# Turning attention probabilities by DMA transposes of 16-bit halves instead of TensorE transposes, for five of sixteen pairs of heads

## The chip, the cores and the metric

The kernel runs on one core of one Trainium2 chip. The metric is the device time of one execution in microseconds; the median of the two runs shown is 601.02 us (600.94 and 601.1). The core has five engines that run side by side, each in its own program order: TensorE (PE, with its weight loads PEld), VectorE (DVE), ScalarE (ACT), GpSimd (POOL) and SyncE (SP, which here only issues DMAs). They wait for one another by semaphores.

## The reference

One layer of a hybrid diffusion trunk: 1024 latent tokens and 128 prompt tokens of width 1024, in float32. After a normalised, modulated input projection there are two groups of heads. The part that the change touches is the attention of the latent tokens, which read 1024 latent keys and 256 cached context keys in one softmax:

```python
def one_block(i):
    s0 = i * Q_BLOCK
    qn = lax.dynamic_slice_in_dim(q_nope, s0, Q_BLOCK, axis=1)
    logits = []
    for qr, (kn, kr, _) in zip(q_ropes, key_sets):
        qrb = lax.dynamic_slice_in_dim(qr, s0, Q_BLOCK, axis=1)
        logits.append(jnp.einsum('bqhn,bkhn->bhqk', qn, kn)
                      + jnp.einsum('bqhr,bkr->bhqk', qrb, kr))
    s = jnp.concatenate(logits, axis=-1).astype(jnp.float32) * ATTN_SCALE
    p = jax.nn.softmax(s, axis=-1).astype(v_all.dtype)
    return jnp.einsum('bhqk,bkhv->bqhv', p, v_all)
```

The group's output is gated, joined with the other group's, multiplied by the output projection w_o, added to the input under a gate and normalised.

## The kernel before

The kernel is one stream of stages: modulation and input projections (to about 315 us of the span), attention (to about 510 us), output projection and normalisation (to the end). Matmuls are done in three passes on float32 values split into a high part (rounded to float32r by ScalarE or GpSimd) and a low part (the rest, a subtraction on VectorE: lo_of, line 112).

**Attention.** There are 8 tiles of 128 queries and 4 heads, in 16 pairs of heads (pair 0 is tile 0, heads 0 and 1; pair 6 is tile 3, heads 0 and 1; pair 10 is tile 5, heads 0 and 1). The loop at line 2006 runs over c. In iteration c, TensorE does the scores of pair c + 1 (score_steps, line 1511) and, woven into them, the value products of pair c - 1 (value_steps, line 1593). A score-only stretch and a value stretch are merged by planned costs (merged, line 212), so that TensorE always has the one while the other's helpers work.

For one head, scores lie in PSUM as 128 queries x 1280 keys (tile s, two buffers, one for each head of a pair). softmax (line 1453) takes maxima on VectorE (L1463 over 1024 columns, L1466 over 256), exponentials on ScalarE into e (L1481), and lets GpSimd multiply e by 1/sum (L1486). The value product contracts over keys, so e must be turned: tr(i) (L1609) transposes four 128x128 blocks of e on TensorE into a PSUM tile pT, five times for a pair (10 blocks of keys x 2 heads). ScalarE copies pT rounded into ph (L1613), VectorE subtracts to get pl (L112), and av(i) (L1633 to L1635) multiplies ph and pl by the values, with tr two steps ahead of av (LAG). e has 6 buffers, ph and pl 4 each, os (the copied value sum) 2.

**Who else works there.** In iterations up to c = 9 GpSimd also forms sums of w_o blocks in tile traw (t_unit, line 1921; L790, four subtractions in an iteration), ScalarE and VectorE split them (L1932, L112), and SP stores the pieces to a DRAM buffer tdram (L1928) and loads the next (L1919). From c = 10 on, SP loads whole pieces of w_o (wo_piece, line 1691; L1705) whose high part GpSimd makes (L115). The first five go through buffers of their own, the last three into buffers of e, so they wait until the turned e of an early enough head is read.

**What sets the order.** The order on each engine is written out: later(dt, fn) puts a piece of work into a list at a planned time, and need(key) runs the list on until that work has been written. No engine reorders anything; if a helper is late, the instructions behind the waiting one on the same engine are late too.

## Time and profile before

| | |
|---|---|
| median of the runs | 601.02 us |
| profiled execution | 600.68 us |
| its span (first to last instruction) | 598.9 us |
| PE busy in the span | 588.7 us (98%) |
| DVE, ACT, POOL busy | 428.7, 329.7, 213.5 us |
| mean granted TensorE clock | 0.997 |
| DMA | 67.33 MB, mean 112 GB/s |

The profiled execution's time is 1.8 us above its span: what lies around the first and last instruction. It is 0.34 us below the median of the runs.

A row of the timeline gives start, duration, engine, line, operation, tiles written and read, and shapes; "x4" merges four. Matmul durations overlap, as the array is pipelined: what one costs is the distance to the next start. The attention iterations of the middle begin, by the first score matmul of each, at 370.0, 381.9, 393.7, 405.6, 417.5, 429.3, 441.2, 453.0 and 464.8 us of the span; these are c = 5 to c = 13.

### The profile page before, as it was taken

How to read it: one execution, taken by the hardware profiler on the slowest of the kernel's cores; microseconds unless marked ns; L12 is line 12 of the kernel's file. 1: busy time of each engine (PE TensorE's matmuls, PEld its weight loads, DVE VectorE, ACT ScalarE, POOL GpSimd, SP SyncE). 2: the span in 40 equal slices, each digit the busy share in tenths (PEclk: the TensorE clock that was granted, in tenths of full speed). 3: DMA queues.
4: the chain of work that ended last, by engine and by line, in shares of the span. 5: the costliest groups of instructions: out<-in, count | busy, mean ns of one | idle time of the engine just before them, and what ended most of it. 6: DMA issues, size and time to landing. Idle time of an engine off the chain costs nothing.

```text
span 598.9 us, 10175 instructions
## 1 busy us (share of the span) xinstructions
PE 588.7 (98%) x3653; PEld 527.0 (88%) x3653; DVE 428.7 (72%) x946; ACT 329.7 (55%) x771; POOL 213.5 (36%) x251
## 2 busy tenths in 40 slices
PE   8999999999999999999999999999999999999995
PEld 7578889999999999999998888888888898888884
DVE  3676888967647467476678677778788876477885
ACT  6665886434323245455567556655756462457543
POOL 2562103200000000343264345454543547269834
PEclk9999999999999999999999999999999999999998
DMA  8991002051050134100002033434242019951444
GB/s 314 366 378 74 1 4 68 1 210 71 7 207 26 45 96 138 42 1 0 2 8 71 0 106 111 156 123 142 85 144 90 1 71 307 359 178 39 140 153 161
DMA packets 31059, 67.33 MB, mean 112 GB/s; under 512 B 3344, under 2 KB 17440, under 8 KB 29984
## 3 DMA queue, kind: packets, MB, share of 16 engines
q1 hardware_dynamic: 27792, 55.93, 26.7%
q0 software_dynamic: 2352, 8.39, 4.1%
q10 hardware_dynamic: 864, 2.36, 1.2%
q8 instruction: 29, 0.48, 0.3%
q14 instruction: 22, 0.18, 0.1%
HBM read 53.45 MB, written 13.21 MB: 111 GB/s over the span
## 4 chain that ended last, share of the span: by engine, by line
PE 92%; DMA 3%; POOL 2%; DVE 1%; ACT 1%; issue 0%; SPq 0%; POOLq 0%; ACTq 0%
PE p L928 15%; PE tp L949 7%; PE pT L1609 5%; PE o L1633 3%; PE o L1635 3%; PE o L1634 3%; PE zacc L1372 2%; PE zacc L1371 2%; PE zacc L1373 2%; PE S L1970 2%; PE S L1971 2%; PE S L1972 2%; DMA ada<-in_ada_ss 2%; PE s L1526 2%; PE s L1529 2%; PE s L1528 2%
## 5 line engine op out<-in xcount | busy, mean ns | idle before, releaser
L1486 POOL TENSOR_SCALAR e<-e,rs 128x1280 f32<-128x1280 f32 x32 | 47.0, 1470 | 96.8 <-DVE rs L1485 64.7
L112 DVE TENSOR_TENSOR pl<-pT,ph 128x512 fp32r<-128x512 f32 x81 | 55.5, 686 | 32.8 <-ACT ph L1613 32.6
L1481 ACT ACTIVATE e<-s,nb,scl 128x256 f32<-128x256 f32 x64 | 56.9, 891 | 38.8 <-DVE nb L1469 26.2
L1613 ACT CAST ph<-pT 128x512 fp32r<-128x512 f32 x80 | 47.2, 590 | 40.6 <-PE pT L1609 40.3
L1219 POOL TENSOR_TENSOR kr<-z,rope 128x64 f32<-128x64 f32 x8 | 2.6, 326 | 154.6 <-ACT z L1228 154.6
L949 PE MATMUL tp<-area,w 128*128 128x384 f32 x288 | 52.5, 337 | 0.0
L1633 PE MATMUL o<-ph,vh 128*128 128x256 f32 x160 | 50.7, 317 | 0.0
L949 PEld LDWEIGHTS tp<-area,w 128*128 128x128 f32 x288 | 50.4, 188 | 0.0
L1609 PE MATMUL pT<-ident,e 128*128 128x128 f32 x320 | 47.9, 272 | 0.0
L1609 PEld LDWEIGHTS pT<-ident,e 128*128 128x128 f32 x320 | 38.9, 140 | 7.2
L1635 PE MATMUL o<-ph,vl 128*128 128x256 f32 x160 | 45.1, 282 | 0.0
L1634 PE MATMUL o<-pl,vh 128*128 128x256 f32 x160 | 44.8, 280 | 0.0
L1463 DVE TENSOR_REDUCE m<-s 128x1 f32<-128x1024 f32 x32 | 38.9, 1216 | 2.6 <-PE s L1504 2.5
L1633 PEld LDWEIGHTS o<-ph,vh 128*128 128x128 f32 x160 | 30.2, 188 | 4.7 <-ACT os L1643 2.9
L1634 PEld LDWEIGHTS o<-pl,vh 128*128 128x128 f32 x160 | 30.3, 189 | 0.4
L1635 PEld LDWEIGHTS o<-ph,vl 128*128 128x128 f32 x160 | 30.1, 188 | 0.0
L928 PE MATMUL p<-area,w 128*128 128x384 f32 x144 | 27.6, 337 | 0.0
L928 PE MATMUL p<-area,s 128*128 128x384 f32 x144 | 27.3, 337 | 0.0
L1371 PE MATMUL zacc<-w1t,area 128*128 128x448 f32 x72 | 27.0, 375 | 0.0
L928 PE MATMUL p<-w1t,s 128*128 128x384 f32 x144 | 26.6, 339 | 0.0
L1372 PE MATMUL zacc<-w1t,area 128*128 128x448 f32 x72 | 26.3, 366 | 0.0
L1373 PE MATMUL zacc<-w1t,area 128*128 128x448 f32 x72 | 26.3, 365 | 0.0
(703 smaller groups left out, 1767.8 us busy)
## 6 DMA issues: line engine op xcount, KB each, us to landing
ada<-in_ada_ss SPq DMA_DIRECT2D x16, 512.0 KB, 8.6
w2r<-in_w_t SPq DMA_DIRECT2D x12, 512.0 KB, 5.3
x<-in_x SPq DMA_DIRECT2D x9, 512.0 KB, 5.6
adag<-in_ada_g SPq DMA_DIRECT2D x4, 1024.0 KB
traw<-in_w_o SPq DMA_DIRECT2D x16, 256.0 KB, 3.0
tdram<-thi SPq DMA_DIRECT2D x32, 128.0 KB, 1.8
tdram<-traw SPq DMA_DIRECT2D x32, 128.0 KB, 1.8
wor<-in_w_o SPq DMA_DIRECT2D x8, 512.0 KB, 3.8
```

What stands on the lines that cost most here:

```text
L112: V.tensor_tensor(lo, src, f32(hi), op=ALU.subtract)
L928: T.matmul(banks[key], a_, b_, start=k == 0 and m == 0, stop=k == 3 and m == len(passes) - 1)
L949: T.matmul(tps[c, 2][:, :GW], w_[c][:, k, :], x_[k, 2], start=k == 0 and m == 0, stop=k == NK - 1 and m == 2)
L1371: T.matmul(ps[:, :448], a, wqh[k], start=k == 0, stop=False)
L1463: V.tensor_reduce(m[:, 0:1], lat_, axis=AX.X, op=ALU.max)
L1481: S.activation(e[:, sl], src, AF.Exp, bias=nb, scale=scl[:, t : t + 1], accum_out=su[:, i : i + 1])
L1486: G.tensor_scalar(e, e, rs, 0.0, op0=ALU.mult, op1=ALU.add)
L1609: T.transpose(ps[:, w : w + P], es[t, h][:, c * P : (c + 1) * P], ident)
L1613: later(0.5, lambda: S.copy(ph[:, :w], ps[:, :w]))
L1633: T.matmul(o, vh[:, kt, :], ph[:, sl], start=c == 0, stop=False)
L1634: T.matmul(o, vh[:, kt, :], pl[:, sl], start=False, stop=False)
L1635: T.matmul(o, vl[:, kt, :], ph[:, sl], start=False, stop=c == n - 1)
```

## The change

For the pairs in CONV, 6 to 10, e is no longer turned on TensorE. When GpSimd has normalised a head's e, it copies e twice more, as 16-bit integers: once the low and once the high halves of the 32-bit words, gathered into a tile b of 128 x 2 x 1280 (to_dram). SP stores b to a DRAM buffer pd. In the next iteration SP issues two DMA transposes of 512 rows x 640 columns of 2 bytes for the pair (from_dram). Since the rows alternate low and high half, the halves of a word stand side by side again after the turn, in a tile raw in SBUF, 128 keys x 10 blocks x 256 queries of two heads in float32. parts(i) then makes ph and pl from raw instead of from pT.

The value products of these pairs move one iteration back: those of pair 6 from c = 7 to c = 8, and so on; those of pair 10 come to c = 12, ahead of those of pair 11. Iteration c = 7 has none. To make room, e goes from 6 to 5 buffers, ph and pl from 4 to 3, os from 2 to 1. raw lies where the first two pieces of w_o went, so their loads move from after the last t_unit to the end of c = 12, behind pieces 2 to 4.

```diff
+CONV = range(6, 11)
...
+    pdram = [gd.tile([2, P, 2, 1280], U16, tag=f"pd{i}", name=f"pd{i}") for i in range(2)]
...
+    def to_dram(t, h):
+
+        both = ap_.tile([P, 1280], F32, tag="b", name=f"b{t}{h}", bufs=2).bitcast(U16).rearrange("p (s c) -> p s c", s=2)
+        words = es[t, h].bitcast(U16).rearrange("p (c s) -> p s c", s=2)
+        for i in range(2):
+            pool_copy(both[:, i, :], words[:, i, :])
+
+        def store():
+            nc.sync.dma_start(pdram[(2 * t + h // 2) % 2][h % 2], both)
+            made.add(("st", t, h))
+
+        later(5.2, store)
+
+    def from_dram(p_):
+        need(*[("st", *pairs[p_][:1], 2 * pairs[p_][1] + x) for x in range(2)])
+        if "raw" not in turned:
+            turned["raw"] = ht.tile([P, 6144], F32, tag="area0", name="raw0")
+        raw = turned[p_] = turned["raw"][:, 2560 * (p_ % 2) : 2560 * (p_ % 2) + 2560]
+        dst = raw.bitcast(U16).rearrange("p (c r) -> p c r", c=10)
+        rows = pdram[p_ % 2].rearrange("h q s c -> (h q s) c")
+        for i in range(2):
+            nc.sync.dma_start_transpose(dst[:, 5 * i : 5 * i + 5, :], rows[:, 640 * i : 640 * i + 640])
...
-        e = ap_.tile([P, 1280], F32, tag="e", name=f"e{t}{h}", bufs=6)
+        e = ap_.tile([P, 1280], F32, tag="e", name=f"e{t}{h}", bufs=5)
...
             made.add(("e", t, h))
+            if 2 * t + h // 2 in CONV:
+                to_dram(t, h)
...
         def tr(i):
+            if 2 * t + pr in CONV:
+                return parts(i)
...
+        def parts(i):
+            src = turned[2 * t + pr][:, 512 * i : 512 * i + 512]
+            ph, pl = pts[i] = tuple(ap_.tile([P, 512], F32R, tag=n_, name=f"{n_}{t}{pr}_{i}", bufs=3) for n_ in ("ph", "pl"))
+            S.copy(ph, src)
+
+            def low():
+                lo_of(pl, src, ph)
+                made.add(("p", t, pr, i))
+
+            later(0.65, low)
...
-            steps.append((0.44, lambda i=i: it[1](i)))
+            steps.append((0.0 if pairs.index(pair) in CONV else 0.44, lambda i=i: it[1](i)))
...
+            if c - 1 in CONV:
+                later(2.0, lambda c=c: from_dram(c - 1))
...
-                merged(sc, value_stream(pairs[c - 1]) if c > 0 else [])
+                merged(sc, [s_ for p_ in range(c) if p_ + 1 + (p_ in CONV) == c for s_ in value_stream(pairs[p_])])
...
+            if c == CONV[-1] + 2:
+                weights_room()
```

GpSimd, at the two heads of pair 6 (e30, e31), before; traw are the w_o blocks, a pair of subtractions to a row:

```order
L1486 TENSOR_SCALAR e30_4251<-e30_4251,rs30_4250 128x1280
L790 TENSOR_TENSOR traw3_4094<-traw3_4094 128x256 x2
L1486 TENSOR_SCALAR e31_4302<-e31_4302,rs31_4301 128x1280
L790 TENSOR_TENSOR traw4_4256<-traw4_4256 128x256 x2
L1486 TENSOR_SCALAR e32_4414<-e32_4414,rs32_4413 128x1280
```

and after:

```order
L1514 TENSOR_SCALAR e30_4253<-e30_4253,rs30_4252 128x1280
L117 TENSOR_SCALAR b30_4325<-e30_4253 128x1280 x2
L793 TENSOR_TENSOR traw3_4096<-traw3_4096 128x256 x2
L1514 TENSOR_SCALAR e31_4304<-e31_4304,rs31_4303 128x1280
L117 TENSOR_SCALAR b31_4399<-e31_4304 128x1280 x2
L793 TENSOR_TENSOR traw4_4258<-traw4_4258 128x256 x2
L1514 TENSOR_SCALAR e32_4423<-e32_4423,rs32_4422 128x1280
```

Two copies stand between a head's normalisation and the w_o subtractions, and so ahead of the next head's normalisation.

SP in the same place, before; thi and traw are the split w_o blocks on their way to DRAM:

```order
L1928 DMA tdram_92<-traw3_4094 128x256 x2
L1928 DMA tdram_92<-thi31_4387 128x256 x2
L1928 DMA tdram_92<-traw3_4094 128x256 x2
L1919 DMA traw5_4419<-in_w_o 128x2x256 x2
L1928 DMA tdram_92<-thi40_4521 128x256 x2
```

and after; pd0 is the DRAM buffer of pair 6, raw0 the tile that its transposes fill:

```order
L1971 DMA tdram_92<-thi31_4392 128x256 x2
L1466 DMA pd0_93<-b30_4325 128x2560
L1971 DMA tdram_92<-traw3_4096 128x256 x2
L1962 DMA traw5_4428<-in_w_o 128x2x256 x2
L1466 DMA pd0_93<-b31_4399 128x2560
L1479 DMA_TRANSPOSE raw0_4524<-pd0_93 128x5x512 x2
L1971 DMA tdram_92<-thi40_4527 128x256 x2
```

The two stores and the two transposes stand in the one queue with the w_o stores, which follow them.

TensorE at the start of iteration c = 7 before: a block of scores of pair 8 (s140), then the turning of pair 6 (pT30), then value products left from pair 5 (o2):

```order
L1526 MATMUL s140_4493<-kch_3227,area1_119 128x512
L1527 MATMUL s140_4493<-kcl_3228,area1_119 128x512
L1528 MATMUL s140_4493<-kch_3227,area1_119 128x512
L1529 MATMUL s140_4493<-krh_3229,area1_119 128x512
L1609 MATMUL pT30_0_4501<-ident_75,e30_4251 128x128
L1609 MATMUL pT30_0_4501<-ident_75,e31_4302 128x128
L1633 MATMUL o2_4259<-ph21_3_4446,vh_3231 128x256
L1634 MATMUL o2_4259<-pl21_3_4447,vh_3231 128x256
```

and after, from the context scores of head 0 (s2) over the halves of both heads (L1563) to head 1 (s141):

```order
L1530 MATMUL s2_3388<-kch_3229,area1_121 128x256
L1531 MATMUL s2_3388<-kcl_3230,area1_121 128x256
L1532 MATMUL s2_3388<-kch_3229,area1_121 128x256
L1533 MATMUL s2_3388<-krh_3231,area1_121 128x256
L1534 MATMUL s2_3388<-krl_3232,area1_121 128x256
L1563 MATMUL s140_4506<-krl_3232,area1_121 128x512
L1563 MATMUL s141_4531<-krl_3232,area1_121 128x512
L1556 MATMUL s141_4531<-kch_3229,area1_121 128x512
```

Iteration c = 7 is scores alone now; the left value products of pair 5 follow in c = 8, behind the first scores of pair 9.

More of the change, by code (lines that the diff above doesn't have):

```diff
@@ L13 @@
 I32 = mybir.dt.int32
+U16 = mybir.dt.uint16
 AF = mybir.ActivationFunctionType
@@ L1956, in open_wo, with weights_room @@
             c_wo, wo = opened("wo", side="left")
+        def weights_room():
+            whole[0] = ht.tile([P, 16, GW], F32R, tag="area0", name="area0b").rearrange("p a c -> p (a c)")
+            flat[0] = [whole[0][:, n * 1024 : (n + 1) * 1024] for n in range(6)]
             for k in range(2):
```

15 lines of the change are left out of this document (8 added, 7 removed).

## The prediction

> **What bounds the kernel now.** I read the page's totals and chain first, then the windows of the attention iterations, then the timelines of single engines.
>
> ```profile
> span 598.9 us, 10175 instructions
> PE 588.7 (98%) x3653; PEld 527.0 (88%) x3653; DVE 428.7 (72%) x946; ACT 329.7 (55%) x771; POOL 213.5 (36%) x251
> PE 92%; DMA 3%; POOL 2%; DVE 1%; ACT 1%; issue 0%; SPq 0%; POOLq 0%; ACTq 0%
> core 0: us, PE busy (x) PEld busy (x) DVE busy (x) ACT busy (x) POOL busy (x), PEclk, DMA share, GB/s
> 393.75:405.62 11.87, 11.87 (x87) 10.49 (x85) 9.03 (x21) 7.42 (x17) 5.85 (x6) 1.00 0.29 98
> 441.20:453.00 11.80, 11.80 (x86) 10.42 (x85) 10.38 (x23) 6.59 (x14) 5.30 (x6) 1.00 0.37 134
> ```
>
> TensorE is the bound: 92% of the chain, and no gap in an iteration of 11.87 us at full clock. So work taken off it counts in full, until a helper is the slower one. VectorE has 9.03 us to do in an iteration, GpSimd 5.85.
>
> **What leaves TensorE.** In the timeline of TensorE (start, duration, engine, line), one step of turning with the value products behind it:
>
> ```profile
> 403.20 0.39 PE L1527 MATMUL s<-kcl,area 128*128 128x512 f32 x1
> 403.43 0.39 PE L1528 MATMUL s<-kch,area 128*128 128x512 f32 x1
> ...
> 403.88 0.60 PE L1609 MATMUL pT<-ident,e 128*128 128x128 f32 x4
> ...
> 404.55 0.28 PE L1635 MATMUL o<-ph,vl 128*128 128x256 f32 x1
> 404.67 0.28 PE L1633 MATMUL o<-ph,vh 128*128 128x256 f32 x1
> ...
> 405.03 0.28 PE L1500 MATMUL s<-kch,area 128*128 128x256 f32 x1
> L1609 PE MATMUL pT<-ident,e 128*128 128x128 f32 x320 | 47.9, 272 | 0.0
> ```
>
> From 403.88 to 405.03 are 1.15 us. Six value matmuls at the distance 0.12 (404.55 to 404.67) take 0.70 of them, so a step of four transposes costs 0.45. The 320 of the group are 16 pairs x 5 steps x 4; five pairs lose 25 steps: **-11.2 us**. That is 1.9%, so even a change without any cost stays just inside the 2% that a measurement of this kernel can tell from no change.
>
> **The empty iteration, c = 7.** It holds only scores: 16 matmuls at 0.23 (403.20 to 403.43), 10 at 0.12 and the halves of 0.66, so 5.5 us. But each head of the next pair needs the score buffer that the same head of the last pair frees with its exponential:
>
> ```profile
> 410.86 0.73 PE L1533 MATMUL s<-krl,area 64*128 64x512 f32 x4
> 416.81 0.20 ACT L1481 ACTIVATION_READ_ACCUMULATOR e<-s,nb,scl 128x1 f32 x1
> 417.37 0.28 PE L1504 MATMUL s<-krl,area 128*128 128x256 f32 x1
> 421.75 0.20 ACT L1481 ACTIVATION_READ_ACCUMULATOR e<-s,nb,scl 128x1 f32 x1
> ```
>
> Head 0 is complete with the halves at 411.5 and its buffer free at 417.0, 5.5 us later; head 1 is complete at 417.5 and free at 421.95, 4.5 later. Now the value products between cover this. Without them the halves of c = 7, due 2.4 us after its start (eight matmuls of 0.23, five of 0.12), wait until 4.5: 2.1 lost. c = 7 then ends 7.6 after its start (4.5 + 0.66 + 2.4), while head 0's buffer is free at 10.65 (5.15 + 5.5), and the first scores of c = 8 stand ahead of any value product: 3.0 more. Between 0, if the helpers, without pT to read, free the buffers that much sooner, and 5.1: I take **+4**, near the measured latencies.
>
> So, by TensorE alone, c = 12 would start at 393.7 + 5.5 + 4 + 4 x 9.6 (11.87 less five steps) = 441.7, where it was 453.0; c = 12 holds the values of pair 10 as well and takes 4.1 us more (0.7 and the rest of its five steps).
>
> **GpSimd.** Its rows in one iteration, and VectorE's beside the second e:
>
> ```profile
> 382.54 1.34 POOL L1486 TENSOR_SCALAR e<-e,rs 128x1280 f32<-128x1280 f32 x1 [3.26 <-DVE rs L1485]
> 383.84 1.56 POOL L790 TENSOR_TENSOR traw<-traw 128x256 f32<-128x256 f32 x2
> 388.01 1.62 POOL L1486 TENSOR_SCALAR e<-e,rs 128x1280 f32<-128x1280 f32 x1 [2.61 <-PE s L1533]
> 389.60 1.56 POOL L790 TENSOR_TENSOR traw<-traw 128x256 f32<-128x256 f32 x2
> 387.73 0.69 DVE L112 TENSOR_TENSOR traw<-traw,thi 128x512 fp32r<-128x512 f32 x1
> L115 POOL TENSOR_SCALAR area<-wor 128x512 fp32r<-128x512 f32 x12 | 7.3, 624 | 3.9 <-DMA wor<-in_w_o 3.9
> L790 POOL TENSOR_TENSOR mixB<-mixA 128x512 f32<-128x512 f32 x4 | 5.2, 1301 | 0.0
> ```
>
> A copy of 1280 16-bit integers is in no row. By elements it is like e's 1.34, same operation and count. By bytes it is 640 floats, 0.75 by the L115 row. Were it as slow per element as a subtraction of two tiles (1.301 for 512), it would take 3.25. I take 1.34. A pair then needs 2 x 1.34 + 4 x 0.78 + 4 x 1.34 = 11.2 us.
>
> The second e takes 1.62, beside a VectorE subtraction with both inputs in SBUF: 0.28 more. An iteration has two such now (traw). The change adds five, as pl is made from raw and ph, both in SBUF, where it was pT in PSUM. So a pair costs GpSimd 11.7 in c = 5 and 6, and 13.1 from c = 8. From 382.5 its queue ends with pair 6 at 394.2, pair 7 (due at 394.4) at 406.1, pair 8 at 419.2, pair 9 at 432.3, pair 10 (its second head has no w_o subtractions, -1.6) at 443.8. ScalarE (L1932) and SP's stores wait behind it; behind L1932 on ScalarE stand exponentials and ph, so TensorE is slowed before the data are missed.
>
> **Store and transposes.** Each is 640 KB (128 x 2560 x 2 bytes; 512 x 640 x 2 bytes).
>
> ```profile
> GB/s 314 366 378 74 1 4 68 1 210 71 7 207 26 45 96 138 42 1 0 2 8 71 0 106 111 156 123 142 85 144 90 1 71 307 359 178 39 140 153 161
> wor<-in_w_o SPq DMA_DIRECT2D x8, 512.0 KB, 3.8
> kvg<-in_kv_g SPq DMA_DIRECT2D x1, 64.0 KB, 6.8
> ```
>
> At the w_o load's rate 640 KB take 4.75 us. A transpose is in no row: between 1.7 (378 GB/s, the busiest slice) and 68 (ten times the 64 KB load of 6.8, the slowest for its size). I take 4.75, nearest to it in size and shape. Pair 10's first half then is there at 443.8 + 2 x 4.75 = 453.3. It is needed one us after c = 12 starts, as leftovers of pair 9 come first. So c = 12 starts at 452.3, not 441.7: **+10.6**, in which the helpers' waits of c = 8 to 11 are contained. With no collisions and the same copies the queue ends at 437.5, and the term is 4.3; with copies of 0.75 it is 0. On one queue SP moves the w_o stores and loads behind these DMAs; the loads are an iteration ahead and tdram is read from 495 on, so I cost that at nothing; if GpSimd is over 11 us late, that cover is gone and its own subtractions wait.
>
> The Trainium skill (VectorE: DVE Perf Modes, section The three transpose paths) gives 1309 ns for one 128 x 128 block of 2-byte values by DMA against 390 on TensorE; 20 blocks in turn would be an estimated 26 us. No run here shows it yet.
>
> **The end.** e has five buffers, so the w_o piece 6 now reuses one of pair 14's and waits with piece 7 for the last turning:
>
> ```profile
> 499.94 0.33 SPq L1705 DMA_DIRECT2D wor<-in_w_o x1
> 501.59 1.65 POOL L115 TENSOR_SCALAR krh<-wor 128x512 fp32r<-128x512 f32 x2
> 506.31 0.48 PE L1999 MATMUL w<-krh,area 128*128 128x512 f32 x1
> 507.17 1.21 POOL L115 TENSOR_SCALAR area<-wor 128x512 fp32r<-128x512 f32 x2 [3.93 <-DMA wor<-in_w_o]
> ```
>
> Piece 7, issued at 499.94, arrives at 507.17. Piece 6 (krh) would arrive then, be copied by 507.8 and split by 508.8, where TensorE uses it at 506.31: **+2.5**, between 0 (it comes sooner, with nothing ahead of it) and 5 (two pieces share the time). Three ph and pl suffice for two steps ahead, one os for a copy that TensorE reads before the next: nothing; if not, a step waits about 0.7.
>
> **Sum**, on the profiled execution's 600.7 (0.3 under the median): -11.2 + 4 + 10.6 + 2.5 = +5.9, **606.6 us**. With the GpSimd term between 4.3 and 16 (half way to that of the second rival) this case spans 600 to 612.
>
> **The rivals.**
>
> *GpSimd keeps up*: copies of 0.9 us or less, so that its pair fits into 9.6. Then VectorE, 10.38 us in the later window against 9.6, costs about 1, and the sum is -11.2 + 4 + 1 + 2.5 = -3.7: 597. For it: GpSimd's idle 6 us. Against it: e's 1.34 for as many elements. With a smaller hole and end it reaches 590.
>
> *The port is held whole* (slower). In another place a subtraction of SBUF tiles starts inside a GpSimd copy:
>
> ```profile
> 443.00 1.20 POOL L115 TENSOR_SCALAR area<-wor 128x512 fp32r<-128x512 f32 x2
> 443.65 1.10 DVE L112 TENSOR_TENSOR area<-wor,area 128x512 fp32r<-128x512 f32 x1 [0.62 <-POOL area L115]
> ```
>
> It takes 1.10, not 0.69, ending about 0.55 after the copy. If the two never run together, GpSimd's pair grows by all seven subtractions, 11.2 + 7 x 0.69 = 16.0 (12.5 in c = 5 and 6): its queue ends at 454.0, c = 12 starts at 462.5, +20.8 in place of 10.6: 617. It decides from about 14.7 a pair. Against it: e lost 0.28, not 0.69. The Trainium skill (SBUF — State Buffer, section SBUF: two separate sides) calls the port pair that VectorE and GpSimd share an exclusive lock for a whole instruction; by it the sum would be this rival's. The two rows above do not contradict it.
>
> *The transposes are slow* (slower). They follow one another on one queue: pair 6's can start at 399, pair 10's first is the ninth, so 399 + 9 x T must be 453: T up to 6.0 us hides behind GpSimd. Each us more costs 9: 615 at 7, 642 at 10. It also holds SP's other DMAs.
>
> *It costs nothing*: -11.2 and about 1 for VectorE, 590.5; only with no hole, or gaps that shrink, is it below 589.
>
> **Chances.** Forecast 0.37, GpSimd keeps up 0.27, port held whole 0.15, slow transposes 0.18, over 2% faster 0.03. Slower by over 2% (above 613): 0.12 of the port's, 0.17 of the transposes', 0.03 of the forecast's upper end, 0.32. Faster 0.03. Within 2% the rest, 0.65. The range of 593 to 628 leaves out the better part of the clean case (0.08) and transposes over 8.5 us (0.11).
>
> **What would show it.** Right: the group of turned pT has 220, not 320; TensorE idle in c = 7 and at the start of 8, waiting for ScalarE; the 16-bit copies near 1.34 and GpSimd over 90% busy from about 395 to 444; waits of ScalarE for traw and raw before c = 12; a gap before w<-krh near the end. Wrong: copies under 0.9 and no wait for raw (GpSimd keeps up), pl from raw at over 1.2 us each (port), or raw's DMAs landing over 6 us after issue with SP waiting on them (transposes).

## The result, and the profile after

The changed kernel takes 640.04 us (median of 2 runs, 639.44 to 640.64) against 601.02: the ratio is 1.065, with a 95% interval of 1.063 to 1.067. The forecast was 606.6 us, with a range of 593 to 628. The change is slower by 39 us, and the forecast fell short by 33.

From the page of the changed kernel: span, busy times, the granted clock of TensorE by slices, the chain's shares, and two groups (busy us, mean ns of one, and behind the second bar the idle time ahead of the group and what ended it).

```profile
span 637.6 us, 10050 instructions
PE 595.4 (93%) x3553; PEld 527.9 (83%) x3553; DVE 436.8 (69%) x947; ACT 332.4 (52%) x771; POOL 243.4 (38%) x271
...
PEclk9999999999999999999999999887896999999999
...
PE 70%; DMA 12%; DVE 8%; POOL 3%; ACT 3%; issue 2%; SPq 2%; ACTq 0%; POOLq 0%
...
L1641 PE MATMUL pT<-ident,e 128*128 128x128 f32 x220 | 33.1, 273 | 0.0
L117 POOL TENSOR_SCALAR b<-e 128x1280 uint16<-128x1280 uint16 x20 | 27.2, 1378 | 17.9 <-DMA pd<-b 17.5
```

The 100 transposes are gone (220 in the group, not 320), and yet TensorE is busy 6.7 us longer than before. Its share of the chain falls from 92% to 70%; what comes in is first DMA (from 3% to 12%) and VectorE (from 1% to 8%). Two things show at once that no row of before had: GpSimd waits 17.5 us for the stores to free its two buffers b, and TensorE's granted clock drops in slices 26 to 31.

The windows of the changed kernel from the halves of one iteration to those of the next, c = 7 to 12 (columns: length and sum, then busy us of TensorE, its weight loads, VectorE, ScalarE, GpSimd, the granted clock, the DMA share and GB/s):

```profile
399.40:412.90 13.50, 10.70 (x49) 8.19 (x48) 9.76 (x19) 7.86 (x16) 10.46 (x10) 0.87 0.78 207
412.90:429.20 16.30, 11.67 (x65) 9.85 (x64) 9.06 (x17) 6.30 (x13) 11.41 (x10) 0.90 0.70 188
429.20:450.90 21.70, 12.88 (x65) 10.48 (x64) 10.52 (x23) 9.07 (x21) 11.51 (x10) 0.84 0.80 227
450.90:467.20 16.30, 13.32 (x65) 11.05 (x64) 10.79 (x18) 7.11 (x14) 11.30 (x9) 0.79 0.87 261
467.20:491.00 23.80, 15.56 (x91) 13.80 (x90) 13.82 (x24) 8.85 (x18) 8.54 (x9) 0.78 0.65 175
```

Each was 11.87 us before (the last now holds part of two pairs' value products). The five are 1.6, 4.4, 9.8, 4.4 and 11.9 longer, 32 of the 39 us together; the rest comes behind them. TensorE is idle for 27.5 us of these 91.6. What it is busy is also stretched by the clock: busy time times the missing share of the clock (10.70 x 0.13 + 11.67 x 0.10 and so on) gives an estimate of 11 us.

SyncE's queue in the changed kernel, the time between one pair's transposes and the next (start, duration with waiting, what):

```profile
420.70 6.20 SPq L1479 DMA_TRANSPOSE raw<-pd  x2
...
430.06 0.40 SPq L1466 DMA_DIRECT2D pd<-b  x1
430.55 1.40 SPq L1971 DMA_DIRECT2D tdram<-traw  x2
433.90 1.22 SPq L1962 DMA_DIRECT2D traw<-in_w_o  x2
435.17 0.60 SPq L1466 DMA_DIRECT2D pd<-b  x1
439.96 2.68 SPq L1479 DMA_TRANSPOSE raw<-pd  x1
```

The two transposes keep SyncE for 6.2 us. Then come w_o's stores and loads and the store of the next pair's first head, 8.2 us, with SyncE standing for two of them until the stores to tdram have landed. Then 0.6 for the second head's store, and 4.2 until it has landed and the next transposes can go. That is 19.3 us for a pair, where an iteration of TensorE was to be 9.6. The other pairs' transposes follow at distances of 20.4, 15.3 and 19.1 us.

Who waits for whom, in the changed kernel from 370 to 520 us (total, times, longest):

```profile
ACT thi L1975 <- POOL traw L793: 18.7, 5, 7.1
ACT ph L1660 <- DMA raw<-pd: 18.7, 4, 6.3
POOL b L117 <- DMA pd<-b: 17.5, 5, 7.2
...
PE s L1530 <- ACT e L1509: 12.2, 5, 5.4
```

ScalarE stands in order at w_o's thi and at ph; the exponentials behind them come late; TensorE waits for the score buffers that the exponentials free.

The chain of work that ended last goes, in the stretch of SyncE's rows above, through these transfers (start, time until landing or until what they held up went on):

```profile
420.70 5.71 DMA raw<-pd
431.01 2.83 DMA tdram<-traw
435.17 4.78 DMA pd<-b
439.96 6.25 DMA raw<-pd
```

Between the first two stand ScalarE's ph, exponentials and VectorE's pl; between the next two the reload of traw, which must wait until the old piece is stored, and which stands ahead of the store of b in SyncE's queue. From 395 to 490 us the landing of the stores of b, of the transposes and of w_o's stores makes 22, 18 and 6.5% of the chain, 44 us of the 95.

### The profile page after: what moved, and what is told of

Its sections match the earlier page's. It is cut to its first block, busy times and chain, and to the rows that moved or that the text cites. A ratio compares the mean times of both kernels' runs of the same rounds, so it can differ in the third digit from the quotient of the medians.

```text
span 637.6 us, 10050 instructions
## 1 busy us (share of the span) xinstructions
PE 595.4 (93%) x3553; PEld 527.9 (83%) x3553; DVE 436.8 (69%) x947; ACT 332.4 (52%) x771; POOL 243.4 (38%) x271
## 4 chain that ended last, share of the span: by engine, by line
PE 70%; DMA 12%; DVE 8%; POOL 3%; ACT 3%; issue 2%; SPq 2%; ACTq 0%; POOLq 0%
PE p L931 14%; PE tp L952 7%; DMA pd<-b 3%; DMA raw<-pd 3%; PE pT L1641 2%; PE zacc L1375 2%; PE zacc L1374 2%; PE zacc L1376 2%; PE S L2018 2%; DMA ada<-in_ada_ss 2%; DVE pl L114 2%; PE S L2019 2%; PE S L2017 2%; DVE m L1491 2%; PE o L1676 2%
## 5 line engine op out<-in xcount | busy, mean ns | idle before, releaser
L114 DVE TENSOR_TENSOR pl<-pT,ph 128x512 fp32r<-128x512 f32 x56 | 38.2, 685 | 22.1 <-ACT ph L1645 22.0
L1645 ACT CAST ph<-pT 128x512 fp32r<-128x512 f32 x55 | 32.3, 588 | 33.1 <-PE pT L1641 32.0
L1677 PE MATMUL o<-pl,vh 128*128 128x256 f32 x160 | 46.4, 290 | 0.0
L1676 PEld LDWEIGHTS o<-ph,vh 128*128 128x128 f32 x160 | 31.8, 199 | 15.3 <-ACT os L1686 13.2
L117 POOL TENSOR_SCALAR b<-e 128x1280 uint16<-128x1280 uint16 x20 | 27.2, 1378 | 17.9 <-DMA pd<-b 17.5
L114 DVE TENSOR_TENSOR pl<-raw,ph 128x512 fp32r<-128x512 f32 x25 | 19.8, 794 | 19.7 <-ACT ph L1660 19.5
L1641 PE MATMUL pT<-ident,e 128*128 128x128 f32 x220 | 33.1, 273 | 0.0
L1641 PEld LDWEIGHTS pT<-ident,e 128*128 128x128 f32 x220 | 26.4, 140 | 4.9 <-issue 0.4
L1530 PE MATMUL s<-kch,area 128*128 128x256 f32 (+2 forms) x52 | 18.1, 349 | 12.2 <-ACT e L1509 12.2
L1660 ACT CAST ph<-raw 128x512 fp32r<-128x512 f32 x25 | 15.3, 616 | 25.4 <-DMA raw<-pd 18.7
L1556 PE MATMUL s<-kch,area 128*128 128x512 f32 x48 | 22.3, 465 | 6.2 <-ACT e L1509 6.1
```

The lines of the kernel that those rows point to most:

```text
L114: V.tensor_tensor(lo, src, f32(hi), op=ALU.subtract)
L117: G.tensor_scalar(out, in_, 1.0, 0.0, op0=ALU.mult, op1=ALU.add)
L1641: T.transpose(ps[:, w : w + P], es[t, h][:, c * P : (c + 1) * P], ident)
L1645: later(0.5, lambda: S.copy(ph[:, :w], ps[:, :w]))
L1676: T.matmul(o, vh[:, kt, :], ph[:, sl], start=c == 0, stop=False)
L1677: T.matmul(o, vh[:, kt, :], pl[:, sl], start=False, stop=False)
```

## The experiments

Three theories stood at the start: **1**, SyncE's queue (the stores stand behind the transposes, the copies' buffers stay taken, GpSimd stops); **2**, the time that the data need through DRAM; **3**, the amount of GpSimd's work, as the prediction had it. Theories 4 and 5 came from the runs: **4**, the place of the copies in GpSimd's order; **5**, a ring through SyncE's queue (a pair's transposes, w_o's stores, the next pair's stores and their landing) that sets the pace. Ratios are to the kernel before, run on the same chip.

### The parts one by one

**The cuts alone.** No pair is converted; the fewer buffers and the later w_o pieces stay.

```diff
-CONV = range(6, 11)
+CONV = ()
-            if c == CONV[-1] + 2:
+            if c == 12:
```

> No pair is converted; only the buffers are those of the changed kernel (five e, three ph and pl, one os) and the w_o pieces 0 and 1 are loaded at c = 12. This is the price of the cuts alone: the prediction has 2.5 us at the end (0 to 5), so 603.5, between 601 and 606; more than 608 would mean that the missing buffers, and not the DMAs, cost part of the 39 us.

Measured 604.45 us, ratio 1.006 (1.004 to 1.008). The iterations are as before and the loss lies behind them. The buffers are not what costs 39 us.

**The empty iteration alone.** TensorE turns all pairs, but the value products of pairs 6 to 10 come an iteration later. Two pairs' e lie in the idle area0 for it; e, ph, pl and os have their old number of buffers.

```diff
+        if 2 * t + h // 2 in (8, 10):
+            e = turned["raw"][:, 1280 * n_ : 1280 * n_ + 1280]
-            if 2 * t + h // 2 in CONV:
-                to_dram(t, h)
-            if 2 * t + pr in CONV:
-                return parts(i)
-            if c - 1 in CONV:
-                later(2.0, lambda c=c: from_dram(c - 1))
```

> The kernel before, with TensorE's transposes, but the value products of pairs 6 to 10 come one iteration later, as in the changed kernel: c = 7 holds scores alone and c = 12 two pairs' values. No copies, stores or DMA transposes. What it costs over 601 is the hole alone: the prediction put 4 us on it, between 0 and 5.1, so 601 to 606. If the hole explains more (for instance by a lower granted clock after TensorE's pause), 608 or more with a clock below 1.00 behind c = 7.

Measured 612.02 us, ratio 1.019 (1.017 to 1.020): 11.2 us, more than the upper end, and with a lower clock. TensorE's timeline of this kernel in c = 7 and 8:

```profile
397.21 0.39 PE L1534 MATMUL s<-kch,area 128*128 128x256 f32 x1 [0.57 <-ACT e L1515]
...
398.91 0.73 PE L1567 MATMUL s<-krl,area 64*128 64x512 f32 x3 [0.43 <-ACT e L1515]
...
404.46 0.78 PE L1560 MATMUL s<-kch,area 128*128 128x512 f32 x1 [1.93 <-ACT raw L1515]
405.03 0.63 PE L1561 MATMUL s<-kcl,area 128*128 128x512 f32 x1
405.46 0.63 PE L1562 MATMUL s<-kch,area 128*128 128x512 f32 x1
...
408.45 0.39 PE L1561 MATMUL s<-kcl,area 128*128 128x512 f32 x1
408.68 0.39 PE L1562 MATMUL s<-kch,area 128*128 128x512 f32 x1
```

The waits are the predicted ones, for exponentials that free score buffers: 0.57, 0.43 and 1.93 us, 2.9 together. Behind the longest the matmuls come at a distance of 0.43 us (405.03 to 405.46), and four us later at 0.23 again. So the pause is paid for a second time in half the clock: what stands between 404.46 and 408.22 takes 3.8 us, and 2.1 by the distances at full clock. The windows of this kernel from the halves of c = 6 to those of c = 8, and from c = 11 to c = 13:

```profile
388.00:411.40 23.40, 20.46 (x115) 16.45 (x114) 14.80 (x36) 11.82 (x26) 11.17 (x12) 0.93 0.37 121
...
447.20:479.10 31.90, 30.77 (x225) 27.25 (x224) 23.25 (x45) 16.73 (x34) 11.00 (x11) 1.00 0.14 50
```

Twice 11.87 us, less the value products of one pair (11.87 - 5.5 = 6.4), would be 17.4; the first window takes 6.0 more. Twice 11.87 with the 6.4 added would be 30.1; the second takes 1.8 more. Some 2 us come at the end, as with the cuts; the rest is not located.

**The copies alone.** To the cuts, the 20 copies of 16-bit halves are added; nothing is stored, and TensorE turns all pairs.

```diff
-        def store():
-            nc.sync.dma_start(pdram[(2 * t + h // 2) % 2][h % 2], both)
-            made.add(("st", t, h))
-        later(5.2, store)
-            if 2 * t + h // 2 in CONV:
+            if 2 * t + h // 2 in range(6, 11):
                 to_dram(t, h)
```

> The kernel with the cuts alone (TensorE turns all 16 pairs, value products at their old place), with the 20 copies of 16-bit halves added on GpSimd for pairs 6 to 10 and nothing behind them: no stores, no transposes, nobody reads the copies. It prices GpSimd's load by itself, over 604.5 of the cuts alone. By the prediction's step (GpSimd 11.7 to 13.1 us a pair against iterations of 9.6) the queue must here fit into 11.87 us an iteration, so 1 to 6 us: 605 to 610. If GpSimd's load, through the waits of ScalarE for traw, is what makes most of the loss with plain loads (622), it shows here as 612 or more. If the stores and the order of SyncE's queue are it, 604 to 606.

Measured 617.7 us, ratio 1.027 (1.026 to 1.029): 13 us over the cuts. But GpSimd is not full. Its timeline, VectorE's, and three waits of this kernel (between 375 and 490 us):

```profile
412.89 2.48 POOL L117 TENSOR_SCALAR b<-e 128x1280 uint16<-128x1280 uint16 x2
415.33 2.04 POOL L793 TENSOR_TENSOR traw<-traw 128x256 f32<-128x256 f32 x2
417.86 1.34 POOL L1508 TENSOR_SCALAR e<-e,rs 128x1280 f32<-128x1280 f32 x1 [0.49 <-DVE rs L1507]
```

```profile
416.09 0.69 DVE L114 TENSOR_TENSOR traw<-traw,thi 128x512 fp32r<-128x512 f32 x1 [2.66 <-POOL traw L793]
416.70 0.69 DVE L114 TENSOR_TENSOR pl<-pT,ph 128x512 fp32r<-128x512 f32 x1
...
418.05 1.68 DVE L114 TENSOR_TENSOR traw<-traw,thi 128x512 fp32r<-128x512 f32 x1 [0.40 <-ACT thi L1969]
```

```profile
POOL e L1508 <- DVE rs L1507: 36.6, 16, 4.1
...
DVE traw L114 <- POOL traw L793: 10.3, 4, 2.7
ACT thi L1969 <- POOL traw L793: 9.1, 5, 1.9
```

GpSimd waits 36.6 us for the sums of exponentials. What is short is not its time but the place of its subtraction: it stands behind two copies (2.48 us), VectorE stands in order at the piece that it makes (2.66 us), and the pl that TensorE needs (416.70) stands behind that. This was theory 4, and the next run tests it by order alone.

**The copies behind the subtractions.**

```diff
             if units and units[0][0] in traw:
                 n_ = 1
                 paced[0] += 1
                 for i in range(n_):
                     unit_of[0](*units.pop(0), 2.2 * i)
+            if 2 * t + h // 2 in range(6, 11):
+                to_dram(t, h)
```

> The run with the copies alone (617.7), with one difference: on GpSimd the two copies of a head are put behind the two w_o subtractions of the same head, not ahead of them. GpSimd does exactly the same work. Theory 4 (not the amount of GpSimd's work: VectorE and ScalarE stand in order at w_o's subtraction, which the copies delay by 2.5 to 2.8 us, and with them the next exponentials, so that an iteration becomes 14.2 us): 604 to 608, iterations of 11.9 to 12.2. Theory 3 (the amount of GpSimd's work, or its use of the port to SBUF): 615 to 618, as before.

Measured 608.16 us, ratio 1.011 (1.009 to 1.012): the same work on GpSimd costs 3 to 4 us instead of 13. The two waits for GpSimd's traw are no longer among this kernel's. Theory 4 holds for the copies by themselves, and theory 3 has at most the 3 to 4 us.

**The stores as well.** To this kernel the ten stores on SyncE are added.

```diff
             pool_copy(both[:, i, :], words[:, i, :])
+        def store():
+            nc.sync.dma_start(pdram[(2 * t + h // 2) % 2][h % 2], both)
+        later(5.2, store)
```

> Copies behind the subtractions (608.2) and the ten stores of 640 KB on SyncE, no transposes, values from TensorE's turning. The stores are issued in well under 1 us and free the copies' buffers some 4 us later, so nothing should wait: 608 to 611. If the stores' traffic alone delays w_o's (the DMA engines are the limit): 614 or more.

Measured 608.06 us, ratio 1.012 (1.010 to 1.013). The stores cost nothing.

**The transposes alone.** To the cuts, the ten transposes on SyncE are added, from a piece of DRAM that is written once.

```diff
-        rows = pdram[p_ % 2].rearrange("h q s c -> (h q s) c")
+        rows = pdram[0].rearrange("h q s c -> (h q s) c")
...
+            if c == 6:
+                for x in range(2):
+                    nc.sync.dma_start(pdram[0][x], es[2, 2 + x].bitcast(U16).rearrange("p (s c) -> p s c", s=2))
-            if c - 1 in CONV:
+            if c - 1 in range(6, 11):
                 later(2.0, lambda c=c: from_dram(c - 1))
```

> The kernel with the cuts alone (604.5), with the ten DMA transposes issued on SyncE in c = 7 to 11 as in the changed kernel, from a piece of DRAM written once in c = 6; nobody reads what they bring. TensorE turns all pairs. If holding SyncE's queue is the cost by itself (a): w_o's loads and stores come 6 us later each iteration and the waits of GpSimd for traw's loads grow: 612 or more. If the cost comes only where somebody waits for raw or for the copies' buffers (b): 604 to 608, with each pair of transposes issued in about 6.2 us.

Measured 605.37 us, ratio 1.008 (1.005 to 1.010): 1 us over the cuts, which the two intervals do not tell from none. SyncE's queue in it:

```profile
424.13 7.05 SPq L1478 DMA_TRANSPOSE raw<-pd  x2
...
435.29 6.51 SPq L1478 DMA_TRANSPOSE raw<-pd  x2
```

The transposes hold SyncE as long as in the changed kernel or a little longer (6.4 to 7.5 us a pair, against 5.8 to 6.3). They and w_o's traffic pass through it at distances of 11.2 to 15.8 us a pair, and yet TensorE idles only 0.3 us between 393.75 and 453.0. So holding the queue costs next to nothing while nobody waits for what the transposes bring. The load on the DMA engines is not the cost by itself either: their share in these iterations is 0.71 to 1.00, as high as in the changed kernel's windows above.

### The parts in the chain

**Plain loads in place of the transposes.** The bytes, the copies and the stores stay in number and size; what is left out is the turn, so the values of five pairs are not the reference's. One wait is left out too: a transpose needs the stores of both heads, a plain load here only that of its own head.

```diff
-            pool_copy(both[:, i, :], words[:, i, :])
+            pool_copy(both[:, i, :], words[:, 1, :])
-            nc.sync.dma_start_transpose(dst[:, 5 * i : 5 * i + 5, :], rows[:, 640 * i : 640 * i + 640])
+            nc.sync.dma_start(dst[:, 5 * i : 5 * i + 5, :].rearrange("p c r -> p (c r)"), pdram[p_ % 2][i].rearrange("q s c -> q (s c)"))
```

> The changed kernel with plain loads of the same 640 KB in place of the transposes (the high halves are copied twice, so that what is loaded are finite numbers; the values of five pairs are then not the reference's). All copies, stores, waits and buffers stay. Theory 1 (SyncE is held by the issue of a transpose, about 3 us each): SyncE's issue falls to under 0.2 us, the stores go at once, 602 to 612 us, close to the prediction's sum of 606.6. Theory 2 (latency): the same direction, but only as far as the loads land earlier, 620 to 630. Theory 3 (GpSimd's work): 636 to 640, since GpSimd does exactly the same.

Measured 621.97 us, ratio 1.034 (1.032 to 1.037). The first load of the last pair, for example, takes SyncE 0.38 us and does not wait for the second head's store:

```profile
456.91 0.38 SPq L1479 DMA_DIRECT2D raw<-pd  x1
```

The second goes out at 461.72. So the transposes, together with their wait for both heads, are worth 18 of the 39 us. ScalarE's wait for raw falls from 18.7 to 0.8 us and GpSimd's for the buffers b from 17.5 to 4.6, but ScalarE's for traw stays at 14.0 (it was 18.7). The other 21 us stay with transfers that hold no queue, so theory 1 in its bare form is not the whole.

**Both: plain loads, and the copies behind the subtractions.** The diffs are those of the run above and of the reordering.

> The changed kernel with plain loads for the transposes and the copies behind the subtractions (the values of five pairs are then not the reference's). By the parts measured so far: 601, hole and cuts 11, copies behind 4, less 11.2 of TensorE: 605, between 603 and 611; against the changed kernel with copies behind (640) that would put 30 us on the transposes themselves. If it stays at 618 to 622, the copies' place matters only while TensorE does the turning, and the waits for raw's round trip through DRAM pace the iterations whatever fetches it.

Measured 622.47 us, ratio 1.037 (1.033 to 1.040). The order that gave back 9.5 us while TensorE did the turning gives nothing here. The next run says the same with the transposes in.

**The changed kernel with the copies behind.**

> The changed kernel with the same reordering alone: copies behind the w_o subtractions. Theory 4 gives back what the copies' place costs, about 13 us as far as SyncE's queue does not then hold the buffers anyway: 624 to 634. Theory 1 (SyncE's queue holds GpSimd, whatever the order): 636 to 642. Theory 3: no change, 640.

Measured 639.91 us, ratio 1.064 (1.062 to 1.065): no change. Its ScalarE waits for raw longer than the changed kernel's (between 385 and 505 us):

```profile
ACT ph L1660 <- DMA raw<-pd: 28.8, 4, 12.8
```

What was given back at w_o's subtraction is waited for at raw.

**GpSimd issues the stores.**

```diff
-        def store():
-            nc.sync.dma_start(pdram[(2 * t + h // 2) % 2][h % 2], both)
-            made.add(("st", t, h))
-        later(5.2, store)
+        G.dma_start(pdram[(2 * t + h // 2) % 2][h % 2], both)
+        made.add(("st", t, h))
```

> The changed kernel, but GpSimd itself issues the stores of the halves right behind its copies, so that they no longer stand in SyncE's queue behind the transposes; the transposes stay on SyncE. Theory 1 (SyncE's queue: each pair of transposes keeps SyncE 6 us, the stores behind them go late, the two buffers for the copies stay taken, GpSimd stops): GpSimd's 17.5 us of waiting for those buffers go below 5, and 640 falls to 604 to 618 us, what is left being the transposes' own latency and the hole of c = 7. Theory 2 (the transposes' latency itself makes the data late, whoever issues the stores): 632 to 640. Theory 3 (GpSimd's own work is too long, as the prediction had it): the same or more than 636, GpSimd over 90% busy.

Measured 631.08 us (median of three, 628.83 to 635.42), ratio 1.051 (1.046 to 1.056). The same with the copies behind:

> The reordering and the stores issued by GpSimd. Theories 1 and 4 together: the hole (8), the cuts (3.5) less 11.2 leave 602, and what the transposes' latency and the granted clock after TensorE's pauses add: 605 to 618. If the transposes' own latency sets the pace (theory 2): 628 or more.

Measured 634.88 us, ratio 1.052 (1.048 to 1.057). They give 9 and 5 us back, and by theory 1 in its bare form it should have been over 20: it is refuted a second time. In SyncE's queue of the latter kernel the transposes have become slower:

```profile
415.21 16.43 SPq L1476 DMA_TRANSPOSE raw<-pd  x2
```

This is the slowest of five pairs (6.25 us for the first transpose, 10.15 for the second); the others took 6.8 to 8.3, where the changed kernel has 5.8 to 6.3. GpSimd issued stores of b at 415.75 and 423.35, so that they ran beside it; that they are the reason is not shown.

**The mends of the empty iteration and of the buffers.** To the kernel above: half of pair 5's value products move into c = 7 (pair 6's e lies in the half of raw that is idle until c = 8), and w_o's pieces 5 and 6 use the copies' buffers.

```diff
+                if c == 6:
+                    vs, kept = vs[: len(vs) // 2], vs[len(vs) // 2 :]
+                merged(sc, kept if c == 7 else vs)
-            r = ap_.tile([P, 1280], F32, tag="e", name=f"wor{k}", bufs=5)[:, :1024]
+            r = ap_.tile([P, 1280], F32, tag="b" if k < 7 else "e", name=f"wor{k}", bufs=2 if k < 7 else 5)[:, :1024]
```

> As the run above, and further: c = 7 gets half of pair 5's value products (pair 6's e lies in the idle half of raw meanwhile, so that pair 5's can stay), and w_o's pieces 5 and 6 use the two buffers of the copies, not of e. If the hole and the cuts are what the shifted kernel and the kernel with the cuts alone made them, this takes 5 to 9 us off the run above: 598 to 610. No gain would mean that the waits for raw and traw, not the empty iteration, pace c = 7 and 8.

Measured 633.22 us, ratio 1.052 (1.048 to 1.055): no gain clear of the noise. In this kernel the empty iteration is not what is waited for. (With w_o's stores on ScalarE, below, the same two mends do gain 7 us.)

**Half an iteration more time for raw.** To the changed kernel with the copies behind: each pair's value products are split behind the third step and begin half an iteration later.

```diff
-            nc.sync.dma_start_transpose(dst[:, 5 * i : 5 * i + 5, :], rows[:, 640 * i : 640 * i + 640])
+            later(5.5 * i, lambda i=i: nc.sync.dma_start_transpose(dst[:, 5 * i : 5 * i + 5, :], rows[:, 640 * i : 640 * i + 640]))
...
+                if c in range(8, 12):
+                    n_ = cut[pairs[c - 2]]
+                    vs, kept[:] = kept + vs[:n_], vs[n_:]
+                elif c == 12:
+                    vs = kept + vs
```

> The changed kernel with the copies behind (639.9), with the value products of pairs 6 to 10 another half iteration later (the second transpose of a pair is issued 5.5 us later, since its half of raw is still being read). Same copies, stores, transposes, loads. If raw's own latency sets the pace (theory 2), half an iteration of some 7 us more hides a good part of ScalarE's 28.8 us of waiting for raw: 612 to 628. If rings of in-order queues do, time is not what is short: 634 to 650.

Measured 638.49 us, ratio 1.062 (1.060 to 1.064). ScalarE's wait for raw (between 385 and 510 us):

```profile
ACT ph L1660 <- DMA raw<-pd: 25.6, 6, 7.0
```

It hardly falls against the 28.8 of the same kernel without the delay. So it is not a fixed delay, which more time would have hidden, at least for the first transpose of a pair (the second goes out later too). Theory 2 falls with this, and with the early splitting below, where the same transposes leave little of the wait. That the data come later as the iterations do points to a ring.

### Where the ring is closed

**The splitting of w_o out of the way.** In the changed kernel, w_o's pieces are split at twice the pace, so that this work ends before most of the converted pairs.

```diff
-                n_ = 1
+                n_ = 2
```

> The changed kernel, with the splitting of w_o (loads, GpSimd's subtractions, ScalarE's thi, the stores to tdram) done in twice the pieces per head, so that it has ended before most of the converted pairs. That takes w_o's subtractions off GpSimd, the waits for traw off ScalarE, and the w_o traffic out of SyncE's queue; the two transposes per pair and the copies' stores stay there. Theory 1 (SyncE's queue, in which the stores wait behind the transposes and behind w_o's stores): from 640 to 612 to 625. Theory 2 (transposes' latency alone): 635 or more. Theory 3 (GpSimd's own work): GpSimd's pair falls from 13 to about 9 us, so all of its share goes: 610 to 620, with GpSimd's waits for the copies' buffers unchanged in number.

> The control for it: the kernel before with the same doubled pace of the w_o splitting. Every theory expects little, 599 to 606, since in it no engine but TensorE is short; what it differs from 601 is to be taken off the reading of the run above.

> Both edits at once on the changed kernel: GpSimd issues the stores, and the w_o splitting is early. What is left are the hole of c = 7 (8 us by the shifted kernel), the cuts (3.5) and the transposes' latency, less the 11.2 of TensorE: theory 1 expects 602 to 612. Theory 2 (latency of the transposes sets the pace whatever the queues do): 625 or more.

Measured 626.06 us with the changed kernel, ratio 1.041 (1.039 to 1.043), 615.07 with the kernel before, 1.022 (1.020 to 1.024), and 621.86 with the stores on GpSimd as well, 1.034 (1.033 to 1.036). The control missed its expectation by far: w_o's splitting at that pace costs the kernel before 14 us, most of them ahead of the converted pairs. Even so the changed kernel gains 14 by it. Between kernels that both have the early splitting, the conversion costs 11 us (626 against 615), and 7 with GpSimd's stores, not 39. SyncE's queue of the changed kernel with this edit, and two of its windows:

```profile
407.59 5.85 SPq L1479 DMA_TRANSPOSE raw<-pd  x2
...
420.27 5.56 SPq L1479 DMA_TRANSPOSE raw<-pd  x2
...
430.97 5.66 SPq L1479 DMA_TRANSPOSE raw<-pd  x2
```

```profile
409.00:420.30 11.30, 8.88 (x51) 6.99 (x50) 8.86 (x15) 5.88 (x14) 7.99 (x7) 1.00 0.84 233
420.30:431.60 11.30, 10.21 (x65) 8.66 (x64) 9.29 (x18) 6.48 (x13) 9.44 (x7) 1.00 0.83 232
```

Without w_o's traffic between them the transposes of the first four pairs are 10.7 to 12.7 us apart, not 15.3 to 20.4, the iterations shown take 11.3 us, and the clock stays at 1.00 in them. Between 385 and 505 us ScalarE's wait for traw is 1.1 us and for raw 6.3 (18.7 each in the changed kernel), and GpSimd's for the buffers b is gone. The chain between 395 and 490 us has 8 us of DMA, not 44. Iterations of 11.3 us are shorter than the 11.87 with TensorE's turning, and still longer than the 9.6 that TensorE's own work would need. The three kernels also differ in where the first wait falls, so the 11 and 7 are not a price by themselves.

**w_o's stores on ScalarE.** In the changed kernel with the copies behind, only the eight stores a pair to tdram leave SyncE's queue.

```diff
-                    nc.sync.dma_start(f32(tdram[m - 1, :, k, part_, 256 * c : 256 * c + 256]), src[:, j % 2, :])
+                    nc.scalar.dma_start(f32(tdram[m - 1, :, k, part_, 256 * c : 256 * c + 256]), src[:, j % 2, :])
-                store(i, 1, half)
+                later(1.2, lambda: store(i, 1, half))
-                    t_load(u + 2)
+                    later(1.25, lambda: t_load(u + 2))
-                    open_wo()
+                    later(1.25, open_wo)
```

> The changed kernel with the copies behind the subtractions (639.9), and the eight stores of w_o's pieces per pair issued by ScalarE, which has 5 us to spare in an iteration. SyncE's ring per pair shrinks from 19 us to the store's landing (4.9), the transposes (6) and w_o's loads (1.2), about 12 to 13 us. If that ring sets the pace (theory 5): 610 to 622. If raw's own latency, through ScalarE's waits in front of ph, sets it: 632 or more, with the waits of ScalarE for raw unchanged.

> The same, with half of pair 5's value products in c = 7 and w_o's pieces 5 and 6 in the copies' buffers. With the ring gone, hole and cuts are what is left (8 and 3.5): 3 to 9 us less than the run above, 602 to 615. If it does not fall, c = 7 and 8 are paced by the arrival of raw and not by the missing value products.

Measured 646.68 us, ratio 1.077 (1.074 to 1.079), and with the two mends 639.3, 1.064 (1.062 to 1.065). SyncE's queue and ScalarE's timeline of the first, in the same stretch (the row of two stores goes from the start of the one to the end of the other):

```profile
428.12 6.66 SPq L1479 DMA_TRANSPOSE raw<-pd  x2
```

```profile
430.60 4.45 ACTq L1971 DMA_DIRECT2D tdram<-traw  x2
435.09 0.62 ACT L1660 CAST ph<-raw 128x512 fp32r<-128x512 f32 x1 [5.15 <-DMA raw<-pd]
```

Theory 5 in the form that SyncE's queue alone is the ring falls: with w_o's stores gone from it, the transposes are still 12.4 to 20.6 us apart. Each of the two stores takes ScalarE 0.33 us, but the second starts 4.1 us after the first, and what stands behind it on ScalarE is late; what holds it back the profile does not name. In the chain between 395 and 490 us the landing of the stores of b falls to 6%, while the transposes rise from 18 to 30%.

No kernel here beats the 601 us of before.

**What stays open.** Shown are the parts and their prices, that the chain of the changed kernel goes for 44 of 95 us through landing transfers, and that these nearly leave the chain when w_o's splitting is out of the way. Which single wait sets the pace is not settled: taking away the copies' place, the stores' queue, w_o's stores on SyncE or half an iteration of raw's delay moved the total by +7 to -9 us, and each time another wait took over. Nor is it settled how much of the 25 us that the kernel with early splitting still loses comes from the early splitting, and how much from the conversion. A kernel that moves the whole splitting behind the converted pairs was not tried.

## Why the prediction was wrong, point by point

*TensorE's -11.2 us.* The group has 220 transposes, as said. But the gain is never collected: TensorE was the bound only as long as the helpers kept its pace.

*The empty iteration, +4 (0 to 5.1).* The mechanism and the place were right, waits of 0.57, 0.43 and 1.93 us for exponentials. The term was too small, in part because the step had no price for the clock: the shifted kernel lost 6.0 us there, of which 2.9 are waits and some 1.7 the clock, and 11.2 in all. In the changed kernel this term is mixed with others: mending it, together with the end, gained nothing with GpSimd's stores and 7 us with w_o's stores on ScalarE.

*GpSimd, +10.6.* The copy was sized right: 1.33 us in the kernel with the copies alone, 1.38 in the changed one, for the 1.34 assumed. That the term's size lies near that kernel's 13 us is luck, since its reason was wrong. The step summed GpSimd's work to 13.1 us a pair and let the queue run full; the page shows GpSimd waiting, and the same copies behind the subtraction cost 3 to 4. What failed is the step from a sum of busy times to a lateness: the order on GpSimd counts, because VectorE and ScalarE wait in order for one of its results. The sign to look for, over 90% busy, did not come: 77, 70 and 53% in the first three windows above.

*SyncE at nothing.* "The loads are an iteration ahead and tdram is read from 495 on, so I cost that at nothing": this is the step that failed most. For the pieces alone it holds, 1 us for the transposes and none for the stores. In the changed kernel SyncE's order ties the next pair's store to w_o's stores, these to ScalarE's thi and GpSimd's subtractions, and those to the copies' buffers that the store frees. Once they are late, the cover is gone, as the same sentence warned, and the time that this costs had no term. The sum counted one store and two transposes, those of the last pair; in the chain that ended last ten transfers stand between 395 and 490 us, of the stores, of the transposes and of w_o's stores, 44 us together.

*The transposes, 4.75 us each.* One was issued in about 3 us (6.2 for two), nearer to the assumed value than to the 10 of the rival that gave 642. That the rival's 642 lies near the 640 is luck: it let the transposes follow one another with nothing between them. In the changed kernel 15.3 to 20.4 us pass from a pair's transposes to the next, 18.5 on average, two thirds of it w_o's traffic, the stores and their landing. Half of that, put for T into the rival's formula, gives 606.6 + 9 x 3.25 = 636; but this explains nothing, since there is one pair of transposes in an iteration and their distance is the iteration's length, whatever makes it long. By the estimate from the Trainium skill (VectorE: DVE Perf Modes, section The three transpose paths) 20 blocks would have taken 26 us; no transpose here took that long, and the 6.2 us for 40 blocks are 155 ns a block.

*The end, +2.5.* The cuts alone cost 3.5, in the predicted stretch, but as four waits of 0.3 to 0.5 us for the last w_o pieces and small shifts, not as one gap.

*The port held whole.* The prediction set a rule of the Trainium skill (SBUF — State Buffer, section SBUF: two separate sides) against a row in which e lost 0.28 us and not 0.69. That row was misread. VectorE's subtraction had begun 0.28 before e (387.73 and 388.01), so only 0.41 of it lay beside e. In the kernel with the copies alone a subtraction beside e took 1.68 instead of 0.69 us (418.05 to 419.73), ending 0.53 after e did at 419.20: it looks as if most of it ran only when e was over. These rows agree with the rule roughly, not to the hundredth: e lost 0.28 of 0.41, and 0.53 is less than 0.69. The rival's sign did not come, though: pl from raw takes 0.79 us on average in the changed kernel, not over 1.2. And GpSimd's added copies, port included, are worth 3 to 4 us once their order is right, in a kernel without pl from raw.

*The sum.* By measured parts it would be 601 + 11 (shift, with most of the cuts) - 11 (TensorE) + 4 to 13 (copies) + 1 = 606 to 615, near the forecast. The measured 640 is 25 to 34 more. So the terms were not far off together, and adding them was the error: in the changed kernel they are waits of engines and transfers that wait for each other.

## What to carry to other kernels

Work that leaves the bounding engine for helpers is not priced by the helpers' busy time. Follow one piece of data through every in-order queue that it passes, with what stands ahead of it there and what that waits for; if the path comes back to where it began, add it up as a ring and compare it with the iteration. Here 15.3 to 20.4 us stood against 9.6. Such a sum is a warning and not a price: no run here shows that one link of the ring sets the pace, and each link that was taken out left another. And before a unit is slowed by a missing input, price the clock as well: in the shifted kernel 2.9 us of TensorE's waits cost 6.0.

## What the runs showed of the hardware

**The clock can fall after a pause of two microseconds.** Windows of the changed kernel behind pauses of 2.25 and 2.38 us (the last figure but two of a row is the granted clock):

```profile
420.43:422.43 2.00, 2.00 (x5) 1.61 (x6) 1.72 (x6) 0.00 (x0) 1.64 (x2) 0.50 0.10 23
422.43:424.43 2.00, 2.00 (x11) 1.87 (x10) 0.00 (x0) 0.00 (x0) 1.92 (x3) 0.72 1.15 223
427.74:429.74 2.00, 2.00 (x14) 1.83 (x15) 1.09 (x4) 2.00 (x4) 0.00 (x0) 1.00 1.02 303
```

The first pause was followed by some 3 us at half the clock, the second by none. The Trainium skill (TensorE: Matmul & The Clock Gate, section Part 1: The HAM clock gate (the "warmup" mystery)) has the half clock after an idle window of about 3.4 us and the full one after as long a busy one, in windows that run freely. The length of the slow stretch agrees with that; that a pause of 1.93 us was enough in the shifted kernel does not.

**A DMA transpose held its queue for about 3 us.** A transpose of 640 KB kept SyncE for about 3 us in the changed kernel (6.20 for the two shown above), a plain load of as many bytes for 0.38 (shown above, in the kernel with plain loads). With the stores on GpSimd's queue it was up to 10.15 for one, 16.43 for two. With TensorE's turning and nobody waiting for the data, two took 6.4 to 7.5.
